# A fused encoder step: gelu and silu as single ScalarE functions, 48 loads moved to another queue, two streams of side work at other steps

## The chip, the cores and the metric

The kernel runs on one core of one Trainium2 chip. A core has five engines with their own instruction streams: TensorE (PE in the profile; its weight loads stand apart as PEld), VectorE (DVE), ScalarE (ACT), GpSimd (POOL) and SyncE (SP, which here only issues DMAs). Each engine works off its own stream in order; semaphores tie the streams together. The metric is the device time of one launch, in microseconds, as the median of several runs.

## The reference, cut to what matters

One layer of an encoder for 2048 frames of a new stream and 64 frames of a running one, 2112 token columns in all, in float32. Two branches are merged, and a feed-forward part with a short convolution follows:

```python
xn = rmsnorm(x, norm_mix);  proj = xn @ w_in          # 1024 -> 5632
x_rnn, y_gate, q, k, v, g_rnn, g_attn = split(proj)
xc = causal_dwconv(x_rnn)                             # width 4
h  = rg_lru(xc)                                       # gates, scan over positions
y_rnn  = h * gelu(y_gate)                             # jax's gelu: the tanh form
y_attn = band_attention(rope(q), rope(k), v, sinks)   # window of 128, chunks of 64
x = x + (sigmoid(g_rnn) * y_rnn + sigmoid(g_attn) * y_attn) @ w_out
up = rmsnorm(x, norm_ffn) @ w_up                      # 1024 -> 2 * 2816
gate, val = split(causal_dwconv(up))                  # width 3
x = x + (silu(gate) * val) @ w_down                   # 2816 -> 1024
y = rmsnorm(x, norm_final)                            # and the new caches and states
```

## The kernel before, in words

Data lies transposed: 128 channels on the partitions, tokens along the columns. All matrix products are made of three passes over a split operand: a float32 value is cut into a rounded high part (ACT, line 200 in `split`) and the remainder (DVE, sometimes POOL, line 201), and high*high, high*low and low*high are accumulated in PSUM. So each 128x128 piece of weights costs three matmuls per block of tokens, and each operand costs an ACT and a DVE instruction.

There are four stages.

- **Recurrent and attention stage.** The tokens are cut into three sets of two blocks (320, 384 and 352 columns). For each set all 44 column groups of `w_in` are multiplied (lines 226 to 228). In set 0 the weights come raw and are split, and the parts are kept in DRAM (`wiS`); sets 1 and 2 load them ready. Per set four attention groups run, and beside each of them two of the eight channel tiles c of the recurrent branch: `rnn_x`, `rnn_y`, the gates (`rnn_gates`), `rnn_scan`, `rnn_g`, `rnn_a`. `rnn_y` takes the product for `y_gate` out of PSUM (line 584) and makes the gelu by hand: Square on ACT (586), two DVE instructions (587, 588), Tanh on ACT (589), one more on DVE (590). The factor 1/2 of the gelu is taken later, in `mix` (620). PSUM has three buffers `mm` for the products of this stage, shared with the gates.
- **Output projection.** `wout` runs over three pairs of token blocks (304, 304 and 448 columns) and eight output tiles m. Each m needs two half tiles of `w_out` (in the first pair raw and split, then stored to `woS` by POOL's queue; in the other pairs loaded from `woS` by SP's queue) and the residual rows `xres` (line 797), four buffers of which are in turn. `residual` adds the product to them and stores them by POOL's queue to `x1S` (line 815). The buffer of m+2 is that of m, so its load waits until the store of m has landed. Beside it run `mixes` (the next pair's operand, line 774) and `xprep` (line 735).
- **Up projection.** Seven products replace eight in a Strassen form; a step is one product u of one feature tile g, in one or two lanes (pairs of token blocks). There are 140 steps with two lanes of 304 columns each (called the shared stretch here), 14 steps each for pair 0 and pair 1 alone, and 77 steps with pair 2 at 448 columns. `Lane.after` takes the sums out of PSUM, runs the convolution on ACT and DVE, and two steps later `gate` makes silu by hand: Tanh on ACT (1070), one DVE instruction over all columns (1074), and one that multiplies with the value half (1076, 1079). From step 10 on, one piece of side work per step is drawn from `fill`: `xsums` (the operand sums of pair 2, to `xS`) and then `wsums` (the weight sums of feature tiles 10 and 21, to `wuS`).
- **Down projection.** Again seven products i, each over three token pairs p and 11 pieces k. The weights of product i+1 are loaded, summed and split while product i runs; `draws(i + 1)` does one of the 11 pieces. It is called at p == 1 for k 0 to 3 and at p == 2 for k 0 to 6.

The program is written in one order, and a list scheduler reorders it for each engine before it is compiled; what it gives is fixed and is shown below for the places of interest. Tiles live in hand-managed regions (`FW`, `RA`, `RE`, `FA`, `FB`, `FD`, ...), which is why the profile names those instead of tiles after the first stage.

Of the kernel before, what the change touches and what calls it, by code (L numbers as in the profile page):

```python
# [7 lines left out]
F32 = mybir.dt.float32  # L8
F32R = mybir.dt.float32r
AF = mybir.ActivationFunctionType  # L10
ALU = mybir.AluOpType
# [3 lines left out]
P = 128  # L15
# [4 lines left out]
EPS = 1e-6  # L20
GC = 0.7978845608028654
G3 = 0.044715

SETS = [[(0, 320), (320, 320)], [(640, 384), (1024, 384)], [(1408, 352), (1760, 352)]]
BN = 384
# [103 lines left out]
def kernel(ctx: ExitStack, tc: tile.TileContext, xT, w_in, w_out, w_up, w_dn, gw, pk,  # L129
                             sinks, cq, sq, ck, sk, kcT, vcT, kcn, vcn, augk, auge, ident_in,  # L130
                             yT, kpT, ksT, vpT, vsT, kc_o, vc_o, h_o, lc_o, fc_o):
    nc = tc.nc
# [216 lines left out]
    for si, blocks in enumerate(SETS):  # L349
# [206 lines left out]
        def rnn_scan(c, st):  # L556
# [8 lines left out]
            nc.vector.scalar_tensor_tensor(a, a, 2.0, tr, op0=ALU.subtract, op1=ALU.mult)  # L565
            nc.scalar.activation(t, t, AF.Sqrt)
            nc.vector.scalar_tensor_tensor(t, t, -1.0, a, op0=ALU.mult, op1=ALU.mult)
            nc.vector.tensor_tensor(ti, ti, t, op=ALU.mult)
            nc.vector.tensor_scalar(a, a, -2.0, -1.0, op0=ALU.mult, op1=ALU.add)
            h = tr  # L570
# [6 lines left out]
        def rnn_y(c, st):  # L577

            w = kept(20 + c, si)
            st["y"] = []  # L580
            for t0, n in blocks:
                ps = proj(w, t0, n)
                y = rp_.tile([P, BN], F32, name="y")[:, :n]
                nc.scalar.activation(y, ps[:, :n], AF.Copy)
                v = rp_.tile([P, BN], F32, name="v", bufs=1)[:, :n]
                nc.scalar.activation(v, ps[:, :n], AF.Square)
                nc.vector.tensor_scalar(v, v, G3, 1.0, op0=ALU.mult, op1=ALU.add)
                nc.vector.tensor_tensor(v, v, y, op=ALU.mult)
                nc.scalar.activation(v, v, AF.Tanh, scale=GC)
                nc.vector.scalar_tensor_tensor(y, v, 1.0, y, op0=ALU.add, op1=ALU.mult)  # L590
                st["y"].append(y)
                yield
# [200 lines left out]
    def wout(i, m):  # L793
        work = []
        for t0, n in phases[i]:
            xr = io[i].tile([P, n], F32, name="xres")
            nc.sync.dma_start(xr, xT[m * P:(m + 1) * P, t0:t0 + n])
            work.append((t0, n, xr, acc()))
# [180 lines left out]
    class Lane:  # L979
# [86 lines left out]
        def gate(self):  # L1066

            n, g, p = self.n, self.g, self.p
            th = self.Gg[:, :self.cols]
            nc.scalar.activation(th, self.ug, AF.Tanh, scale=0.5)  # L1070
            h = up["c"].tile([P, 2 * n], F32, name="hp", bufs=4 if n < BM else 3)

            def mult():
                nc.vector.scalar_tensor_tensor(th, th, 1.0, self.ug, op0=ALU.add, op1=ALU.mult)
                cut = min(TP - self.t0, 2 * n)
                nc.vector.scalar_tensor_tensor(h[:, :cut], th[:, :cut], 0.5, self.uv[:, :cut],
                                               op0=ALU.mult, op1=ALU.mult)
                if cut < 2 * n:
                    nc.vector.scalar_tensor_tensor(h[:, cut:], th[:, cut + 2:], 0.5, self.uv[:, cut + 2:],
                                                   op0=ALU.mult, op1=ALU.mult)  # L1080

# [114 lines left out]

    dweights, dloads, dahead = {}, {}, [1]

    def fetch(j):
# [71 lines left out]
    for i, (lanes, fresh, u) in enumerate(plan):  # L1271
# [139 lines left out]
    for j, (i, p, k, ms, cs) in enumerate(seq):  # L1411
# [14 lines left out]

        if i < 6 and (p == 1 and k < 4 or p == 2 and k < 7):
            draws(i + 1)
# [176 lines left out]
```

## Time and profile before

| what | value |
|---|---|
| median of 3 runs | 3011.54 us (3001.13 to 3014.64) |
| the profiled execution | 3004.97 us, span 3003.1 us |
| busy share of the span | PE 96%, PEld 92%, DVE 72%, ACT 50%, POOL 14% |
| DMA | 595 MB, mean 198 GB/s |
| mean granted TensorE clock | 0.987 |

A row of groups reads: line, engine, operation, out<-in, shapes, count, then busy time in all and the mean of one in ns, then the idle time of the engine just before these instructions and what ended it. A row of waits reads: who waited, what for, total us, how often, the longest. A row of windows gives for a stretch of time the busy us of PE, PEld, DVE, ACT and POOL with the number of instructions, then the granted clock, the share of the DMA engines and GB/s. Matmuls overlap in the profile (each is given some 0.3 us while one starts every 0.14 us), so the number of matmuls that start per us tells more than PE's busy share.

### The profile page before, as it was taken

What the parts mean: (1) busy time and instruction counts of PE and PEld (TensorE: products, weight loads), DVE (VectorE), ACT (ScalarE), POOL (GpSimd) and SP (SyncE); (2) the same over time, 40 slices, a digit from 0 to 9 for tenths busy, and PEclk for the clock granted to TensorE, in tenths of its full rate; (3) what the DMA queues carried; (4) which work ended last, traced back from release to release, by engine and by line L of the source; (5) the groups of instructions that cost most, each with busy time, mean ns of one, the idle gap of its engine ahead of it and who ended that gap; (6) DMA issues with size and microseconds to landing.
All of it is one profiled execution on the core that took longest, in us unless ns stands there. A gap on an engine that the chain in (4) does not pass through costs nothing.

```text
span 3003.1 us, 49277 instructions
## 1 busy us (share of the span) xinstructions
PE 2873.6 (96%) x17640; PEld 2748.7 (92%) x17640; DVE 2157.2 (72%) x4258; ACT 1509.6 (50%) x3424; POOL 421.7 (14%) x607
## 2 busy tenths in 40 slices
PE   8989999999999999998899999999899999899998
PEld 7989888999998999998899989999899999899998
DVE  5398884377786288886578999888676667566766
ACT  4566662356653266664334445555544445334442
POOL 3221112000000000001111433222111111000001
PEclk9999999999999999999999999999999999999999
DMA  7875547544335634437885667555876677976653
GB/s 243 280 234 181 185 138 227 188 137 131 124 116 169 210 129 136 137 107 256 267 265 203 243 235 249 176 188 199 297 236 217 211 225 221 285 219 198 205 145 123
DMA packets 328854, 595.39 MB, mean 198 GB/s; under 512 B 37168, under 2 KB 230688, under 8 KB 311712
## 3 DMA queue, kind: packets, MB, share of 16 engines
q1 hardware_dynamic: 292640, 470.10, 49.8%
q0 software_dynamic: 35968, 122.13, 10.8%
q8 instruction: 139, 2.28, 0.3%
q14 instruction: 107, 0.88, 0.1%
HBM read 400.99 MB, written 191.64 MB: 197 GB/s over the span
## 4 chain that ended last, share of the span: by engine, by line
PE 46%; DMA 8%; issue 6%; DVE 6%; POOL 1%; ACT 1%; SPq 0%; DVEq 0%; POOLq 0%; ACTq 0%
PE mf L1002 4%; PE mf L1001 4%; PE mf L1003 4%; PE mm L226 4%; PE mm L227 4%; PE mm L228 4%; PE mf L1424 2%; PE mf L1425 2%; PE mf L1423 2%; PE mm L1003 2%; PE mm L1001 2%; PE mm L1002 2%; PE mm L1424 1%; PE mm L1425 1%; PE mm L1423 1%
## 5 line engine op out<-in xcount | busy, mean ns | idle before, releaser
L226 PE MATMUL mm<-xh,whl 128*128 128x320 f32 (+2 forms) x2112 | 688.3, 326 | 9.6 <-ACT xh L200 6.4
L227 PE MATMUL mm<-xl,whl 128*128 128x320 f32 (+2 forms) x2112 | 687.0, 325 | 9.0 <-DVE xl L201 4.9
L228 PE MATMUL mm<-xh,whl 128*128 128x320 f32 (+2 forms) x2112 | 683.7, 324 | 0.6 <-POOL whl L201 0.6
L200 ACT ACTIVATE RE<-FW 128x512 fp32r<-128x512 f32 (+2 forms) x555 | 304.4, 561 | 420.8 <-DMA FW<-hS 60.2
L201 DVE TENSOR_TENSOR RE<-FW,RE 128x512 fp32r<-128x512 f32 (+2 forms) x555 | 327.3, 603 | 162.2 <-ACT RE L200 159.9
L227 PEld LDWEIGHTS mm<-xl,whl 128*128 128x128 f32 x2112 | 399.8, 189 | 18.4 <-DVE xl L201 8.2
L226 PEld LDWEIGHTS mm<-xh,whl 128*128 128x128 f32 x2112 | 400.0, 189 | 17.0 <-ACT xh L200 8.8
L228 PEld LDWEIGHTS mm<-xh,whl 128*128 128x128 f32 x2112 | 399.9, 189 | 1.6 <-POOL whl L201 0.9
L1001 PE MATMUL mf<-RA,RE 128*128 128x304 f32 (+1 forms) x608 | 198.9, 327 | 3.5 <-DMA RE<-wuS 2.6
L1424 PE MATMUL mf<-RE 128*128 128x304 f32 (+2 forms) x616 | 197.8, 321 | 1.1 <-DVE RE L201 1.1
L1003 PE MATMUL mf<-RA,RE 128*128 128x304 f32 (+1 forms) x608 | 198.4, 326 | 0.4 <-DVE RE L201 0.4
L1423 PE MATMUL mf<-RE 128*128 128x304 f32 (+2 forms) x616 | 197.3, 321 | 0.6 <-ACT RE L200 0.6
L1002 PE MATMUL mf<-RA,RE 128*128 128x304 f32 (+1 forms) x608 | 197.9, 325 | 0.0
L1425 PE MATMUL mf<-RE 128*128 128x304 f32 (+2 forms) x616 | 196.0, 318 | 0.0
L1001 PE MATMUL mf<-RE 128*128 128x304 f32 (+1 forms) x488 | 159.6, 327 | 10.1 <-ACT FA L1048 5.0
L1002 PE MATMUL mf<-RE 128*128 128x304 f32 (+1 forms) x488 | 159.4, 327 | 0.9 <-DVE RE L201 0.9
L1003 PE MATMUL mf<-RE 128*128 128x304 f32 (+1 forms) x488 | 159.0, 326 | 0.2 <-DVE RE L201 0.2
L1037 DVE SCALAR_TENSOR_TENSOR FW<-FA,pkt,FW 128x608 f32<-128x608 f32 x176 | 146.1, 844 | 14.9 <-ACT FW L1031 14.7
L201 POOL TENSOR_TENSOR gl<-gr,gh 128x256 fp32r<-128x256 f32 x24 | 21.1, 878 | 800.2 <-ACT gh L200 664.1
L1001 PE MATMUL mm<-RE 128*128 128x304 f32 (+1 forms) x392 | 126.7, 323 | 5.5 <-ACT FA L1048 4.1
L1003 PE MATMUL mm<-RE 128*128 128x304 f32 (+1 forms) x392 | 126.0, 322 | 2.9 <-DVE RE L201 2.9
L457 ACT ACTIVATE pr<-S,nm 128x256 f32<-128x256 f32 (+1 forms) x272 | 123.4, 473 | 7.5 <-DVE nm L453 6.0
(341 smaller groups left out, 7287.3 us busy)
## 6 DMA issues: line engine op xcount, KB each, us to landing
whl<-wiS SPq DMA_DIRECT2D x88, 1024.0 KB, 5.1
RE<-wuS SPq DMA_DIRECT2D x104, 512.0 KB, 4.9
wiS<-whl SPq DMA_DIRECT2D x44, 1024.0 KB, 4.8
wuS<-RE POOLq DMA_DIRECT2D x80, 512.0 KB, 4.1
FW<-in_w_up_dram SPq DMA_DIRECT2D x158, 256.0 KB, 3.7
hS<-FA POOLq DMA_DIRECT2D x154, 152.0 KB, 3.8
FW<-hS SPq DMA_DIRECT2D x154, 152.0 KB, 3.3
wraw<-in_w_in_dram SPq DMA_DIRECT2D x44, 512.0 KB, 5.8
```

Of the source, the lines that this page charges most:

```text
L200: nc.scalar.activation(hi, src, AF.Copy)
L201: (lo_eng or nc.vector).tensor_tensor(lo, src, hi.bitcast(F32), op=ALU.subtract)
L226: nc.tensor.matmul(ps[:, :n], wh[:, c], xh[:, k, :n], start=first, stop=False)
L227: nc.tensor.matmul(ps[:, :n], wh[:, c], xl[:, k, :n], start=False, stop=False)
L228: nc.tensor.matmul(ps[:, :n], wl[:, c], xh[:, k, :n], start=False, stop=last)
L1001: nc.tensor.matmul(ps[:, :n], w[:, 0, c], x[:, k, 0], start=first, stop=False, **more)
L1002: nc.tensor.matmul(ps[:, :n], w[:, 0, c], x[:, k, 1], start=False, stop=False, **more)
L1003: nc.tensor.matmul(ps[:, :n], w[:, 1, c], x[:, k, 0], start=False, stop=last, **more)
L1037: nc.vector.scalar_tensor_tensor(uc, G[:, j:j + self.cols], col("fw", 44 * j + m), uc, op0=ALU.mult, op1=ALU.add)
L1423: nc.tensor.matmul(ps[m][:, cs], w[:, 0, c], t[:, 0], start=k == 0, stop=False)
L1424: nc.tensor.matmul(ps[m][:, cs], w[:, 0, c], t[:, 1], start=False, stop=False)
L1425: nc.tensor.matmul(ps[m][:, cs], w[:, 1, c], t[:, 0], start=False, stop=k == 10)
```

## The change

- `rnn_y` keeps only the copy out of PSUM. The gelu is one ACT instruction per block, `Gelu_apprx_tanh`, in place on the copy, written in `rnn_scan` behind the Sqrt. It gives the whole gelu, so `mix` adds without the factor 1/2.
- `gate` calls `Silu` on ACT; the DVE instruction that multiplied tanh + 1 with the gate is gone, and the multiplication with the value half has no factor.
- The residual rows of the output projection are loaded by POOL's queue.
- `fill` is driven at every second step.
- `draws(i + 1)` is called at the 11 places of a list.

```diff
@@ rnn_scan
             nc.scalar.activation(t, t, AF.Sqrt)
+            for y in st["y"]:
+                nc.scalar.activation(y, y, AF.Gelu_apprx_tanh)
             nc.vector.scalar_tensor_tensor(t, t, -1.0, a, op0=ALU.mult, op1=ALU.mult)
@@ rnn_y
                 nc.scalar.activation(y, ps[:, :n], AF.Copy)
-                v = rp_.tile([P, BN], F32, name="v", bufs=1)[:, :n]
-                nc.scalar.activation(v, ps[:, :n], AF.Square)
-                nc.vector.tensor_scalar(v, v, G3, 1.0, op0=ALU.mult, op1=ALU.add)
-                nc.vector.tensor_tensor(v, v, y, op=ALU.mult)
-                nc.scalar.activation(v, v, AF.Tanh, scale=GC)
-                nc.vector.scalar_tensor_tensor(y, v, 1.0, y, op0=ALU.add, op1=ALU.mult)
@@ mix
-                nc.vector.scalar_tensor_tensor(v, rr[:, o], 0.5, v, op0=ALU.mult, op1=ALU.add)
+                nc.vector.tensor_tensor(v, rr[:, o], v, op=ALU.add)
@@ wout
-            nc.sync.dma_start(xr, xT[m * P:(m + 1) * P, t0:t0 + n])
+            nc.gpsimd.dma_start(xr, xT[m * P:(m + 1) * P, t0:t0 + n])
@@ gate
-            nc.scalar.activation(th, self.ug, AF.Tanh, scale=0.5)
+            nc.scalar.activation(th, self.ug, AF.Silu)
...
-                nc.vector.scalar_tensor_tensor(th, th, 1.0, self.ug, op0=ALU.add, op1=ALU.mult)
                 cut = min(TP - self.t0, 2 * n)
-                nc.vector.scalar_tensor_tensor(h[:, :cut], th[:, :cut], 0.5, self.uv[:, :cut],
-                                               op0=ALU.mult, op1=ALU.mult)
+                nc.vector.tensor_tensor(h[:, :cut], th[:, :cut], self.uv[:, :cut], op=ALU.mult)
@@ the loop over the up projection's steps
-        drive(fill, 1)
+        if i % 2:
+            drive(fill, 1)
@@ the down projection
+    DRAWS = [(0, 8), (0, 10), (1, 3), (1, 8)] + [(2, k) for k in (0, 2, 3, 5, 6, 8, 9)]
...
-        if i < 6 and (p == 1 and k < 4 or p == 2 and k < 7):
+        if i < 6 and (p, k) in DRAWS:
             draws(i + 1)
```

How the instructions now stand on the engines is shown at three places.

**ScalarE in set 0, channel tile 4 of the recurrent branch**, from the splitting of the convolution's output (`xch`) to the gates (`tr`, `ti`). Before:

```order
L200 ACTIVATE xch<-xc 128x320
L584 ACTIVATE y<-mm 128x320
L586 ACTIVATE v<-mm 128x320
L589 ACTIVATE v<-v 128x320
L584 ACTIVATE y<-mm 128x320
L586 ACTIVATE v<-mm 128x320
L200 ACTIVATE whl<-wraw 128x1024
L200 ACTIVATE ph<-pt 128x512
L553 ACTIVATE tr<-mm,bah 128x320
```

Now:

```order
L198 ACTIVATE xch<-xc 128x320
L584 ACTIVATE y<-mm 128x320
L566 ACT_TABLE_LOAD
L566 ACTIVATE y<-y 128x320
L584 ACTIVATE y<-mm 128x320
L198 ACTIVATE whl<-wraw 128x1024
L566 ACTIVATE y<-y 128x320
L198 ACTIVATE ph<-pt 128x512
L551 ACTIVATE tr<-mm,bah 128x320
```

The scheduler does not put the gelu behind the Sqrt, as the program is written, but right behind the copy; a load of the function table stands in front of it, and another one in front of the next exponential. Over the whole program the order of ScalarE has 106 such loads, where it had 57.

**SyncE's queue at the start of the output projection's second pair**, and **GpSimd's queue** in the same stage. SP before:

```order
L797 DMA FW<-in_xT_dram 128x304 x6
L735 DMA FW<-x1S 128x304
L797 DMA FW<-in_xT_dram 128x304 x2
L785 DMA RE<-woS 128x2x512
L797 DMA FW<-in_xT_dram 128x304 x2
L785 DMA RE<-woS 128x2x512 x2
```

SP now:

```order
L782 DMA FW<-in_w_out_dram 128x512
L729 DMA FW<-x1S 128x304
L779 DMA RE<-woS 128x2x512 x3
L768 DMA FW<-mixS 128x448
L779 DMA RE<-woS 128x2x512
```

POOL before:

```order
L815 DMA x1S<-FW 128x304 x2
L790 DMA woS<-RE 256x1x512 x2
L815 DMA x1S<-FW 128x304 x22
L815 DMA x1S<-FW 128x448 x14
```

POOL now, at the same place:

```order
L784 DMA woS<-RE 256x1x512
L791 DMA FW<-in_xT_dram 128x304 x2
L809 DMA x1S<-FW 128x304 x2
L791 DMA FW<-in_xT_dram 128x304 x2
L809 DMA x1S<-FW 128x304 x6
L791 DMA FW<-in_xT_dram 128x304 x2
L809 DMA x1S<-FW 128x304 x2
```

The loads of the residual rows (`FW<-in_xT_dram`) stood ahead of the weight loads (`RE<-woS`) on SP; now they stand on POOL between the stores of the rows before them (`x1S<-FW`).

**VectorE at the start of the down projection**: the sums for the second product's weights (1163 and 1165 before, 1154 and 1156 now) among the last sums of the up projection (1087 to 1096 before) and the splits. Before:

```order
L1163 TENSOR_TENSOR FW<-FW 128x512
L201 TENSOR_TENSOR RE<-FW,RE 128x304
L1165 TENSOR_TENSOR FW<-FW 128x512
L1091 TENSOR_TENSOR FB<-FB 128x448
L201 TENSOR_TENSOR RE<-FW,RE 128x304
L1096 TENSOR_TENSOR FB<-FB 128x448
```

Now:

```order
L1154 TENSOR_TENSOR FW<-FW 128x512
L1083 TENSOR_TENSOR FB<-FB 128x448
L1156 TENSOR_TENSOR FW<-FW 128x512
L199 TENSOR_TENSOR RE<-FW,RE 128x304 x2
L199 TENSOR_TENSOR RE<-FW,RE 128x512
L1082 TENSOR_TENSOR FB<-FB 128x448
L1154 TENSOR_TENSOR FW<-FW 128x512
L1087 TENSOR_TENSOR FB<-FB 128x448
```

Two of the 11 pieces now stand ahead of the up projection's last sums (`FB<-FB`), where there was one between them.

More of the change, by code (lines that the diff above doesn't have):

```diff
@@ L20 @@
 EPS = 1e-6
-GC = 0.7978845608028654
-G3 = 0.044715
 SETS = [[(0, 320), (320, 320)], [(640, 384), (1024, 384)], [(1408, 352), (1760, 352)]]
@@ L1069, in gate @@
             th = self.Gg[:, :self.cols]
[L1070 removed]
+            nc.scalar.activation(th, self.ug, AF.Silu)
             h = up["c"].tile([P, 2 * n], F32, name="hp", bufs=4 if n < BM else 3)
             def mult():
[L1074 removed]
                 cut = min(TP - self.t0, 2 * n)
[L1076 to L1077 removed]
+                nc.vector.tensor_tensor(h[:, :cut], th[:, :cut], self.uv[:, :cut], op=ALU.mult)
                 if cut < 2 * n:
[L1079 to L1080 removed]
+                    nc.vector.tensor_tensor(h[:, cut:], th[:, cut + 2:], self.uv[:, cut + 2:], op=ALU.mult)
             def store(o, src):
```

## The prediction

> **What bounds the kernel now.** I read the page's busy shares first, then windows by stage, then what TensorE waited for in each of them, and last the timelines of the queues behind these waits.
>
> ```profile
> PE 2873.6 (96%) x17640; PEld 2748.7 (92%) x17640; DVE 2157.2 (72%) x4258; ACT 1509.6 (50%) x3424; POOL 421.7 (14%) x607
> ...
> 100.00:500.00 400.00, 364.86 (x2339) 345.21 (x2338) 320.34 (x649) 247.64 (x552) 91.32 (x53) 0.98 0.60 197
> 500.00:1350.00 850.00, 842.05 (x5145) 814.15 (x5145) 585.30 (x1392) 475.37 (x1112) 24.60 (x29) 1.00 0.45 148
> 1380.00:1510.00 130.00, 114.72 (x753) 111.61 (x753) 67.61 (x141) 45.28 (x96) 25.16 (x43) 0.94 0.89 296
> 1640.00:1890.00 250.00, 235.93 (x1652) 231.92 (x1651) 226.28 (x422) 128.48 (x304) 100.28 (x182) 0.99 0.69 239
> 1890.00:2080.00 190.00, 190.00 (x1364) 190.00 (x1364) 162.36 (x269) 101.08 (x234) 48.32 (x90) 1.00 0.53 183
> 2545.00:2620.00 75.00, 66.33 (x393) 60.16 (x392) 44.45 (x78) 26.90 (x58) 7.03 (x13) 1.00 0.98 295
> ```
>
> TensorE is the bound, and the change takes no matmul away. So only its gaps can be won or lost. The rows are, from above: set 0 of the recurrent stage (35 us idle of 400), sets 1 and 2 (8 of 850), the first two pairs of the output projection, the shared stretch of the up projection in two parts, and the start of the second down product (8.7 idle of 75). The two parts of the shared stretch run the same matmuls: 1364 in 190 us are 7.18 per us, and the 1652 of the first part would take 230.1 us at that rate. They took 250, so 19.9 us are lost there and nothing in the second part. These are the waits in the four places, in the same order (set 0; from 1395 on in the projection; the first part of the shared stretch; the down product):
>
> ```profile
> PE Y L479 <- DVE pl L201: 14.1, 15, 2.0
> PE mm L550 <- ACT v L586: 7.4, 6, 1.9
> PE mm L550 <- ACT tr L553: 4.6, 6, 1.1
> ...
> PE mm L805 <- DMA RE<-woS: 9.8, 4, 4.6
> PE mf L805 <- DMA RE<-woS: 3.2, 3, 1.9
> ...
> PE mf L1001 <- ACT FA L1048: 4.8, 3, 1.8
> PE mm L1001 <- ACT FA L1048: 4.1, 3, 3.1
> ...
> PE mm L1424 <- DVE RE L201: 6.9, 8, 1.7
> ```
>
> Everything else, some 2800 us, has a TensorE that finds its work ready; an edit there costs nothing as long as the other engines keep ahead.
>
> **Gelu.** These are the rows of the instructions that go, and the table loads:
>
> ```profile
> L587 DVE TENSOR_SCALAR v<-v 128x320 f32<-128x320 f32 (+2 forms) x48 | 20.4, 426 | 22.1 <-ACT v L586 21.7
> L588 DVE TENSOR_TENSOR v<-v,y 128x320 f32<-128x320 f32 (+2 forms) x48 | 28.5, 595 | 0.3
> L590 DVE SCALAR_TENSOR_TENSOR y<-v,y 128x320 f32<-128x320 f32 (+2 forms) x48 | 25.0, 520 | 6.6 <-ACT v L589 5.7
> L586 ACT ACTIVATE v<-mm 128x320 f32<-128x320 f32 (+2 forms) x48 | 22.0, 459 | 0.9 <-DVE y L590 0.7
> L589 ACT ACTIVATE v<-v 128x320 f32<-128x320 f32 (+2 forms) x48 | 24.0, 501 | 26.9 <-DVE v L588 26.8
> L566 ACT ACT_TABLE_LOAD x24 | 30.8, 1283 | 0.4
> ```
>
> VectorE loses 426 + 595 + 520 = 1541 ns per block, 73.9 us over 48 blocks, 24.7 of them in set 0's 16. ScalarE loses the Square (22.0 us); the Tanh becomes a Gelu, whose duration no row shows. Other functions on the same shapes lie within 459 and 501 ns, so I take the Tanh's own 501. The new order has 106 table loads for 57: 49 * 1.283 = 62.9 us more, 40.9 net, all in the recurrent stage. In sets 1 and 2 ScalarE is busy 475 of 850 us and the convolution, the exponentials and the next products hide the loads; if that cover were gone, the loads would fall on TensorE one by one (last rival). In set 0 it depends on the place. Here is channel tile 4, ScalarE first, then TensorE:
>
> ```profile
> 300.93 0.42 ACT L584 ACTIVATE y<-mm 128x320 f32<-128x320 f32 x1
> 301.25 0.43 ACT L586 ACTIVATE v<-mm 128x320 f32<-128x320 f32 x1
> 302.60 0.47 ACT L589 ACTIVATE v<-v 128x320 f32<-128x320 f32 x1 [0.92 <-DVE v L588]
> 302.98 0.42 ACT L584 ACTIVATE y<-mm 128x320 f32<-128x320 f32 x1
> 303.63 0.44 ACT L586 ACTIVATE v<-mm 128x320 f32<-128x320 f32 x1 [0.23 <-DVE y L590]
> ...
> 304.12 0.41 PE L550 MATMUL mm<-xch,gh 128*128 128x320 f32 x1 [1.53 <-ACT v L586]
> ```
>
> The gates wait for a PSUM buffer that the second block's Square frees at 304.07, because it must go to VectorE and back for the first block's `v`, of which there is one buffer. In the new order ScalarE runs copy (to 301.35), table load (to 302.63), Gelu (0.50, to 303.13), copy (to 303.55): the buffer is free 0.5 us sooner. Six such waits make some 3 of the 7.4 us. The gate behind it waits for `tr`; the second Gelu stands in front of it where the Square stood, so its 4.6 us stay.
>
> The 14.1 us of `Y <- pl` are VectorE's backlog: it works 320 of 400 us, from now on 296. If the wait goes like share/(1 - share), 4.0 falls to 2.8, 30%: 4 to 5 us. So I take **8 us less** here. Bounds: all three waits gone (-26); or the load in front of the gates costs in full in set 0 and nothing is won (8 tiles * 1.283 = +10). I am near the small gain because the timeline shows the wait's place.
>
> The Trainium skill (ScalarE: Activation LUTs, What ACT_TABLE_LOAD costs) gives a switch as a load of 1283 ns and a drain of 1380, and asks to batch calls by table set, which this order does not. The trace shows the first figure and not the second:
>
> ```profile
> 191.39 0.62 ACT L436 ACTIVATE D<-qr 128x512 fp32r<-128x512 f32 x1
> 192.03 1.28 ACT L566 ACT_TABLE_LOAD   x1
> 193.32 0.74 ACT L566 ACTIVATE t<-t 128x640 f32<-128x640 f32 x1
> ```
>
> The instruction before ended at 192.01 and the next began 0.01 us behind the load. By the skill's figure the buffer above would come 0.9 us later than before, and the sum would be some 8 us higher; I go by the row.
>
> **Silu.**
>
> ```profile
> L1074 DVE SCALAR_TENSOR_TENSOR FA<-FA,FW 128x608 f32<-128x608 f32 x44 | 34.1, 783 | 1.7 <-ACT FA L1070 1.7
> L1074 DVE SCALAR_TENSOR_TENSOR FB<-FB 128x898 f32<-128x898 f32 x22 | 24.0, 1091 | 0.0
> ```
>
> 58.1 us of VectorE go; the Tanh becomes a Silu of the same shape (I take the same time), and no table load is added in the up projection by the new order. In the shared stretch that is 0.783 us per lane and feature, in 84 matmuls or 11.7 us: 0.067 of VectorE's time.
>
> **The side work.** `xsums` has 40 pieces, the two `wsums` 8 each; with the drawing that finds each empty that is 59 steps, from step 10 to 68, and 59 * 24 / 7.18 = 197 us at the clean rate plus the 20 lost: the lost stretch has just this length. At every second step it ends at step 127, still ten steps (33 us) before the first load of its weights. VectorE's share is 0.855 in the second part and 226.28 / 230.1 = 0.983 per clean us in the first: the side work is 0.13. Halved it is 0.065, and with silu's 0.067 off VectorE stands at 0.855 + 0.065 - 0.067 = 0.853, as in the part that loses nothing. I take **18 of the 19.9 us**; the bounds are 20 and 6 (the third that silu alone gives: 0.067 of the 0.13 + 0.067 that come off, where the halved work only stretches the same waits).
>
> **Residual rows.** 48 loads leave SP. What they did to it:
>
> ```profile
> SPq L797 <- DMA x1S<-FW: 35.9, 13, 6.4
> ...
> 1425.49 8.54 SPq L797 DMA_DIRECT2D FW<-in_xT_dram  x5
> 1437.23 0.56 SPq L785 DMA_DIRECT2D RE<-woS  x1
> ...
> L815 POOL DMA_DIRECT2D x1S<-FW x46: 539/542/667, 1403.5 to 1592.0; - x46
> ...
> DMA to landing us min/median/max: 2.1/4.2/6.5
> ```
>
> SP stood 35.9 us (from 1440 on) behind residual loads that waited for a store, and the weight loads from `woS` queued behind them; TensorE's 13.0 us of waits for `woS` are these. `mixS` and `x1S` loads stay ahead of some, so I take **8 us less**, with 13 as the one bound. On POOL the wait holds up the next stores: per m two store issues, a landing, two load issues. From the first store's issue that is 4.2 + 2 * 0.54 = 5.3 us against 48 / 7.18 = 6.7 us of matmuls per m, and a row comes some 9 us after its buffer's store (two landings and an issue) where two m, 13 us, are allowed. At the longest landing it is 7.6, 0.9 too long, times 16 m: +14, the other bound. Issuing itself adds 48 * 0.54 = 26 us to a POOL that is busy 25 of 130.
>
> **Draws.**
>
> ```profile
> 2515.00:2530.00 15.00, 15.00 (x82) 14.03 (x82) 14.06 (x23) 11.96 (x30) 0.54 (x1) 1.00 0.62 179
> 2590.00:2605.00 15.00, 10.47 (x62) 8.93 (x61) 10.61 (x19) 5.78 (x13) 1.60 (x3) 1.00 1.06 312
> ```
>
> The DMA engines have room at 2515 and none at 2590, where TensorE waits for splits of late tiles. Two of the 11 pieces move forward into the first pair and the rest spreads over 9 more steps' worth, but the bytes are the same and VectorE is full (14.06 of 15) where two pieces go. I take **4 of the 8.6 us of waits**; bounds -8.6 and +4 (two pieces delaying tokens of the first product by about 2 us each; the longest wait in the row is 1.7).
>
> **Sum:** -8 - 18 - 8 - 4 = -38, on the profiled execution's 3004.97 us: 2967. The median of the runs is 6.6 us above that execution; I take part of it: **2969 us**.
>
> **Rivals.**
> 1. *The side work keeps its waits, stretched.* Against it: the second part's zero at the share I work out. For it: ScalarE's copies (L1048) wait for single VectorE instructions, and bursts may do as well. Gain 38 - 12 = 26: 2981. Chance 0.13.
> 2. *The DMA engines, not the queues, limit the output projection and the down product.* Their share is 0.89 and 0.98 there. Then 12 of the 38 go: 2981. The Trainium skill's rule that issuing engines are not separate DMA queues (DMA: Bandwidth & Descriptors) says just this; the 35.9 us are waits for semaphores, though, which it does not cover. Chance 0.17.
> 3. *POOL's queue becomes the chain of the output projection*, +14 for -8: 2991. It decides from a landing of 5.6 us on; the median is 4.2. Chance 0.05; together with 1 and 2, no change, 0.05.
> 4. *Table loads on TensorE's path (slower).* ScalarE also empties PSUM; with three `mm` buffers a product group has 24 matmuls of some 0.15 us, 3.5 us, to spare. If ScalarE falls behind by that at every switch, 62.9 us come on top in place of the 8: 3005 + 63 - 30 = 3038. Against it: the 24 loads for Sqrt and those behind them stand there now and sets 1 and 2 lose 8 us in all. Chance 0.05.
> 5. That the edits do not reach the machine is excluded for the queues by the order; a gelu in other places than written is what I costed.
>
> **How the numbers follow.** The forecast has 0.50, within 12 us of it; 0.05 is for more (all of the bounds: 2942). Range 2942 to 2997: it leaves out rivals 4 and the combined one and a part of 3. What can be told from no change is 0.5%, 15 us: below 2996 counts as faster, which the forecast and rivals 1 and 2 and most of 3 are: 0.86; same 0.09, slower 0.05.
>
> **What would show it.** In the shared stretch 7.1 matmuls per us throughout. In set 0 no wait on `v`, shorter `Y <- pl`. In the projection no wait for `woS` over 2 us, and POOL's stores at most a few us behind the sums. At the down product's second piece fewer waits for splits. It is wrong if table loads appear ahead of TensorE's waits in sets 1 and 2, or if a new wait for the residual sums (L814) appears.

## The result, and the profile after

The changed kernel takes 3027.59 us (median; 3014.18 to 3039.05), the kernel before beside it 3009.61 us (3001.13 to 3019.91). The ratio is 1.0055, with a 95% interval from 1.0038 to 1.0072: slower by half a per cent, where 1.4% less was predicted. The profiled execution took 3021.46 us, 16.5 more than the one of before.

These are the busy line of the page after and its windows by stage, the same five stages as before and the start of the second down product, which now lies some 15 us later:

```profile
PE 2876.6 (95%) x17640; PEld 2765.8 (92%) x17640; DVE 2053.2 (68%) x4048; ACT 1555.0 (51%) x3425; POOL 452.2 (15%) x655
```

```profile
100.00:500.00 400.00, 368.38 (x2365) 351.34 (x2365) 302.68 (x606) 265.41 (x556) 94.61 (x53) 0.97 0.61 201
500.00:1350.00 850.00, 839.49 (x5151) 818.30 (x5150) 550.00 (x1300) 507.70 (x1113) 25.80 (x29) 1.00 0.45 146
1380.00:1510.00 130.00, 110.81 (x727) 107.95 (x726) 62.66 (x130) 42.52 (x90) 40.03 (x70) 0.93 0.84 278
1640.00:1890.00 250.00, 235.56 (x1641) 234.06 (x1639) 210.77 (x397) 122.05 (x295) 97.35 (x178) 0.97 0.66 228
1890.00:2080.00 190.00, 187.86 (x1337) 187.61 (x1336) 153.01 (x256) 103.07 (x240) 49.92 (x92) 0.99 0.54 189
2545.00:2630.00 85.00, 75.14 (x460) 71.04 (x459) 51.97 (x93) 32.41 (x69) 10.11 (x19) 0.98 0.94 281
```

VectorE did become lighter, by 104 us over the program. In the first part of the shared stretch it works 210.77 us in place of 226.28, and yet TensorE gets through no more matmuls there, 1641, where it did 1652 (and 1644 in a second profiled execution of the kernel before); in the part behind it 1337 for 1364 (1365 in that execution). These are the waits of TensorE after, in the places that the prediction speaks of (set 0; the output projection; 1640 to 1890 us of the shared stretch; the second down product):

```profile
PE Y L477 <- DVE pl L199: 13.8, 10, 2.7
PE mm L548 <- ACT tr L551: 3.5, 3, 1.5
PE mm L224 <- ACT xh L198: 3.2, 4, 1.7
...
PE mm L548 <- ACT y L584: 2.0, 2, 1.4
...
PE mm L799 <- DMA RE<-woS: 8.1, 3, 4.1
PE mf L799 <- DMA RE<-woS: 6.9, 3, 3.1
...
PE mf L995 <- ACT FA L1042: 7.5, 2, 4.7
PE mm L995 <- ACT FA L1042: 5.9, 3, 3.9
...
PE mm L1417 <- DVE RE L199: 7.8, 6, 2.4
PE mf L1417 <- DVE RE L199: 2.0, 1, 2.0
```

Of the waits that were to go, only the one on `v` in set 0 is gone (7.4 us; 2.0 for the copy stand in its place). The others are still there. In the shared stretch the waits for the copies out of PSUM are no longer six of 1.5 us on average, but five of 2.7. Where the time lies is seen when the same matmul is looked up in both traces. The table gives the time from the first matmul of a stage to the first of the next (the last row to the end); "again" is a second profiled execution of the kernel before, and the last columns are experiments from below:

| stage, us | before | again | after | silu_only | silu_pad | silu_kept |
|---|---|---|---|---|---|---|
| start and set 0 | 450.9 | 456.2 | 449.8 | 452.4 | 448.6 | 451.3 |
| sets 1 and 2 | 923.6 | 922.5 | 920.0 | 921.7 | 924.5 | 921.2 |
| output projection | 212.8 | 212.7 | 218.0 | 211.0 | 210.8 | 208.7 |
| up projection, steps 0 to 9 | 42.5 | 45.1 | 48.4 | 42.8 | 42.9 | 42.4 |
| steps 10 to 139 (shared stretch) | 455.1 | 456.1 | 460.5 | 459.5 | 455.5 | 446.2 |
| pairs 0 and 1, one lane each | 59.8 | 59.3 | 65.8 | 65.9 | 60.4 | 61.0 |
| pair 2 | 378.0 | 378.3 | 375.7 | 382.1 | 376.9 | 376.8 |
| down projection and end | 476.8 | 478.3 | 477.9 | 480.6 | 476.1 | 476.6 |

Two executions of one program differ by up to 5 us in a stage, so a difference of that size in a single profile proves nothing; what is said below rests on the timed runs, and on what several kernels have in common.

### The profile page after: what moved, and what is told of

It is laid out like the page before. It is cut to its first block, busy times and chain, and to the rows that moved or that the text cites. A ratio compares the mean times of both kernels' runs of the same rounds, so it can differ in the third digit from the quotient of the medians.

```text
span 3019.7 us, 49053 instructions
## 1 busy us (share of the span) xinstructions
PE 2876.6 (95%) x17640; PEld 2765.8 (92%) x17640; DVE 2053.2 (68%) x4048; ACT 1555.0 (51%) x3425; POOL 452.2 (15%) x655
## 4 chain that ended last, share of the span: by engine, by line
PE 59%; issue 14%; DVE 11%; DMA 10%; POOL 3%; ACT 2%; SPq 1%; POOLq 0%; DVEq 0%; ACTq 0%
PE mm L225 8%; PE mm L226 8%; PE mm L224 8%; PE mf L1417 3%; PE mf L1418 3%; PE mf L997 3%; PE mf L1416 3%; PE mf L996 3%; PE mf L995 3%; DMA FW<-mixS 2%; PE mm L995 2%; PE mm L996 2%; PE mm L997 2%; PE mm L1417 1%; PE mm L1418 1%
## 5 line engine op out<-in xcount | busy, mean ns | idle before, releaser
L224 PEld LDWEIGHTS mm<-xh,whl 128*128 128x128 f32 x2112 | 401.9, 190 | 16.5 <-ACT xh L198 10.4
L1031 DVE SCALAR_TENSOR_TENSOR FW<-FA,pkt,FW 128x608 f32<-128x608 f32 x176 | 147.8, 847 | 17.1 <-ACT FW L1025 16.8
L455 ACT ACTIVATE pr<-S,nm 128x256 f32<-128x256 f32 (+1 forms) x272 | 122.8, 464 | 14.3 <-DVE nm L451 14.1
```

The costliest lines, as they stand in the source:

```text
L224: nc.tensor.matmul(ps[:, :n], wh[:, c], xh[:, k, :n], start=first, stop=False)
L1031: nc.vector.scalar_tensor_tensor(uc, G[:, j:j + self.cols], col("fw", 44 * j + m), uc, op0=ALU.mult, op1=ALU.add)
```

## The experiments

All times are medians beside the kernel before on the same chip; before itself lay between 3006.6 and 3009.6. The ratio, with its interval, is what is compared; it is not the quotient of two medians and can differ from it by 0.1%.

| kernel | us | ratio | 95% interval |
|---|---|---|---|
| gelu_only | 3001.48 | 0.9986 | 0.9971 to 1.0002 |
| silu_only | 3020.39 | 1.0043 | 1.0027 to 1.0059 |
| xres_only | 3019.23 | 1.0041 | 1.0021 to 1.0060 |
| fill_only | 3016.03 | 1.0023 | 1.0008 to 1.0038 |
| draws_only | 3004.17 | 0.9995 | 0.9983 to 1.0007 |
| early_loads | 3019.48 | 1.0042 | 1.0026 to 1.0058 |
| silu_pad | 3005.92 | 0.9991 | 0.9978 to 1.0004 |
| after_v2 | 3025.40 | 1.0046 | 1.0031 to 1.0061 |
| before_v2 | 3008.91 | 0.9995 | 0.9985 to 1.0005 |
| silu_skip | 3019.56 | 1.0037 | 1.0023 to 1.0051 |
| all_but_moves | 3010.55 | 1.0004 | 0.9991 to 1.0018 |
| silu_kept | 3001.69 | 0.9981 | 0.9968 to 0.9995 |
| pad_siluorder | 3035.18 | 1.0096 | 1.0077 to 1.0115 |
| all_kept | 2995.16 | 0.9955 | 0.9939 to 0.9971 |
| xres_kept2 | 3016.59 | 1.0033 | 1.0019 to 1.0047 |
| fill_kept | 3024.00 | 1.0062 | 1.0045 to 1.0079 |

**The parts alone.** Each takes one piece of the diff.

> The kernel before with the gelu edit alone. By the stages of the two traces the recurrent stage gained 0.8 us in set 0 and 3.6 in set 1, and lost 0.1 in set 2. Theory 'parts add' (each stage's loss belongs to the edit that touches it): -4 us against before, nothing after 1350 us. Rival 'table loads stand in TensorE's path': +10 or more. Rival 'a reshuffle' (the loss is not tied to an edit, any edit moves waits about): some us in stages that the edit does not touch.

> The kernel before with the silu edit alone: 66 VectorE passes, 58 us, gone. Theory 'late loads' (VectorE, working in order, stands at the side work's own loads; how much else it has to do matters little): the shared stretch gains at most 6 us of the 20 that it loses, and VectorE's waits for x1S stay at 10.6 us or grow. Rival 'VectorE's load' (the forecast's): the stretch gains 6 or more, total -6 to -10, and its waits for x1S stay the same.

> The kernel before with the residual rows' loads on POOL's queue alone. Theory 'POOL's queue holds the stores back': the output projection is 5 us longer (the difference of the two traces there: +1.9, +3.3, +0.1 for the three phases), waits for woS stay at 13 to 15 us. Rival 'the DMA engines limit the stage, whichever queue': 0 to within 2 us. The forecast's step: -8.

> The kernel before with the side work of the shared stretch at every second step alone. Theory 'late loads': each piece still stands at its own load, and the waits that it makes on TensorE are as long or longer and come over twice the steps; +8 to +17 us, nearly all of the loss. Rival 'the loss is of other edits': 0, or the gain of some 10 us that the forecast's term for the side work alone would give.

> The kernel before with the down product's pieces drawn at other steps alone. Theory 'fewer but longer waits': the waits for splits at the second down product go from 8 of at most 1.7 us to fewer of over 2, the sum stays at 8 to 9 us, total -1 to +2. The forecast's step: -4.

Gelu may gain a little (its interval just reaches 1), the draws do nothing that can be told, and the three others lose, silu too, which only takes work away. In per cent the five add to 0.88; together they cost 0.55.

> The kernel before once more, unchanged, for its profile: how far a stage's time and the half-clock time differ between two executions of one program. Theory: stages differ by up to 2 us, the time at half clock by up to 15 us, and the 448-column stage of pair 2 by 0 or 7.5 us. If a stage differs by 5 us or more elsewhere, differences of that size between two kernels' profiles show nothing.

It took 3013.91 us, and its stages stand in the table above. Its set 0 is 5 us longer than in the first profile, and no two other stages differ by 3.

**Two remedies that did not help.** The first: VectorE works its rows in order and stands at a side load that SP issued late; then more steps between load and use should help. One of the four places:

```
                     nc.sync.dma_start(x[o], x1S[kk, :, t + c0:t + c0 + width])
                 yield
+                yield
+                yield
```

> The kernel before, with extra steps inside the side work at one place only: between the issue of its loads and VectorE's first use of them (three steps for one; two for the weights' pieces), and one more between its last stores and the next loads. The work itself, silu and gelu stay as before. Theory 'late loads' (VectorE, in order, stands at a load that SP issued late behind the weights' loads, and the sum that empties PSUM stands behind it): VectorE's waits for x1S and w_up, 10.6 + 3.5 us, fall below 4, TensorE's waits for the copy out of PSUM with them, and the shared stretch gains 5 to 12 us. Rival 'VectorE's load': the same work is done, so only its stretching counts, and since the kernel with the side work at every second step lost 7 us, this is 0 to +5.

It was 0.42% slower. That does not clear late loads of blame, because this edit too moves other rows about (see the end of this section). The second: both lanes share one tile for a copy (`V`), which ties ScalarE to VectorE's addition.

```
-            if u in (0, 1) or u == 2 + (one and self.second_lane):
+            own = one and self.second_lane and "v" in up
+            if u in (0, 1) or u == 2 + (one and self.second_lane and not own):
...
+                up["v"] = Pool(FW)
+                up["v"].reserve("V", BS)
```

> The changed kernel with one thing more: the second lane's copy of X (V) gets a buffer of its own and is made at the third product, as the first lane's, where both lanes shared one buffer and the second lane's copy stood until VectorE had added the first lane's. In all ten profiles taken so far TensorE's waits in the shared stretch stand at one place, the second lane's fifth product, which accumulates into the PSUM bank that this copy reads: 8 to 11 us in sum in the kernels that are not slower there, 16.4 to 19.8 us in silu_only, fill_only, early_loads and the changed kernel. Theory 'the shared copy' (VectorE, in order, stands at a side load or a store ahead of that addition, ScalarE's copy stands behind it, TensorE behind that): the waits at this place fall from 16.6 us to under 4, with half-clock time behind them; 12 to 20 us less than the changed kernel, 3008 to 3015. Rival 'VectorE's loads hold up TensorE by any way': the waits move to the next place (the seventh product), under 5 us in all.

> The kernel before with the same own buffer for the second lane's copy. Theory 'the shared copy': the 8 to 10 us at the second lane's fifth product go, 6 to 10 us less than before. Rival as above: 0 to -3.

> The kernel with silu alone, the buffer still shared, and the side work at every step but the third of a feature, which is the one directly ahead of the addition that frees the shared copy. Theory 'the shared copy': what stands ahead of the addition matters, not how much VectorE works; the waits at the second lane's fifth product fall from 16.7 us to under 8, total 8 to 12 us less than silu_only's 3020. Rival 'in-order waits of one step earlier reach just as far': 15 or more stays.

In the same 250 us, TensorE's waits of after_v2 stand at another place and are as long in sum:

```profile
PE mf L995 <- DVE FA L1050: 10.0, 6, 2.6
PE mm L995 <- DVE FA L1050: 5.7, 3, 2.8
```

With the own buffer alone (before_v2) nothing changes either, 0.9995. The copy was where the lateness showed, not where it came from. Leaving the side work out of one step (`if u != 2: drive(fill, 1)`) did not help either.

> The edits that did not lose alone (gelu, the draws), silu, and the own buffer for the second lane's copy; the residual rows back on SP, the side work at every step. If the four parts add as measured alone (gelu -4 to -7, draws 0 to -4, silu without its loss 0 or a small gain, the own buffer -6 to -10), 2990 to 3000: ahead of both kernels. Rival: silu's loss has another cause, then 3005 to 3012.

With silu in it, nothing is left of what gelu gains.

**The pass put back.** This kernel has silu, and a VectorE pass without effect where silu saves one:

```
             def mult():
+                nc.vector.scalar_tensor_tensor(th, th, 1.0, th, op0=ALU.mult, op1=ALU.max)
                 cut = min(TP - self.t0, 2 * n)
```

> The kernel before with the silu edit and, in the place of the VectorE pass that it saves, another of the same shape that changes nothing (1.0 * th, then the maximum with th). Theory 'a lighter VectorE is slower' (it only comes sooner to its waits for loads and stores, and TensorE's waits gather into fewer, longer ones): back to before, within 3 us. Rival 'ScalarE's Silu costs': stays at +12. Rival 'chance of the state of the last 448-column stage' (that stage ran at 202.7 ns per matmul in one profile and 206.7 in another, 7.5 us in all): +7 or 0, as that stage's rate falls.

It is back at the time of before: 58 us more of VectorE's work make the program 14 us faster than silu_only. The timelines of VectorE show what no count of work shows. First silu_pad, where pair 0's single lane begins at 2085.9, then silu_only, where it begins at 2090.9:

```profile
2093.43 0.47 DVE L1052 TENSOR_TENSOR FA<-mm,FA 128x304 f32<-128x304 f32 x1
...
2094.80 0.47 DVE L1054 TENSOR_TENSOR FA<-mf,FA 128x304 f32<-128x304 f32 x1
...
2098.59 0.48 DVE L1094 TENSOR_TENSOR FA<-FA 128x304 f32<-128x304 f32 x1 [0.27 <-DMA hS<-FA]
```

```profile
2098.15 0.46 DVE L1052 TENSOR_TENSOR FA<-mm,FA 128x304 f32<-128x304 f32 x1
2098.53 0.68 DVE L201 TENSOR_TENSOR RE<-FW,RE 128x512 fp32r<-128x512 f32 x1
2099.13 0.47 DVE L1093 TENSOR_TENSOR FA<-FA 128x304 f32<-128x304 f32 x1
2103.04 0.47 DVE L1093 TENSOR_TENSOR FA<-FA 128x304 f32<-128x304 f32 x1 [3.44 <-DMA hS<-FA]
2103.43 0.47 DVE L1054 TENSOR_TENSOR FA<-mf,FA 128x304 f32<-128x304 f32 x1
```

L1054 is the sum that empties a PSUM bank. In silu_pad it stands ahead of the last in-place sums of `h` (L1094, in silu_only L1093); in silu_only both stand ahead of it, and the second waits 3.44 us for a store of `h` to land. TensorE waits for the sum behind it:

```profile
2103.95 0.41 PE L1001 MATMUL mf<-RD,RE 128*128 128x304 f32 x1 [2.85 <-DVE FA L1054]
```

The program gives both in the same order; it is the scheduler that placed them differently. A piece of VectorE's built order in the shared stretch says the same (`-` silu_pad, `+` silu_only; L935 is the side work's first use of its load, L1052 and L1054 empty PSUM):

```
 L1052 TENSOR_TENSOR FA<-mf,FA 128x304
-L201 TENSOR_TENSOR RE<-FW,RE 128x512 x2
+L935 SCALAR_TENSOR_TENSOR FA<-FA,pkt 128x224
+L201 TENSOR_TENSOR RE<-FW,RE 128x512
 L1052 TENSOR_TENSOR FA<-mm,FA 128x304
-L1085 TENSOR_TENSOR FA<-FA 128x304 x2
-L1054 TENSOR_TENSOR FA<-mf,FA 128x304 x2
-L935 SCALAR_TENSOR_TENSOR FA<-FA,pkt 128x224 x4
+L1084 TENSOR_TENSOR FA<-FA 128x304 x2
+L201 TENSOR_TENSOR RE<-FW,RE 128x512
+L1054 TENSOR_TENSOR FA<-mf,FA 128x304
+L935 SCALAR_TENSOR_TENSOR FA<-FA,pkt 128x224 x3
+L1054 TENSOR_TENSOR FA<-mf,FA 128x304
```

From the output projection to the end of the up projection, silu puts 510 of 1404 VectorE rows at another place in the order, 301 of 1260 on ScalarE, 126 of 436 on POOL and 76 of 525 on SP, as counted in the built programs. (In the traces, where rows of the same form cannot be told apart, 427 of 1395 VectorE rows are seen at another place.) silu_pad moves none, nor do gelu_only and draws_only there.

**The order put back.** To tell the order from the lighter engine, these kernels note the instructions of four queues as the program gives them, and tie each behind the one that stands ahead of it in another kernel's built order:

```
+        for one, two in zip(row, row[1:]):
+            tc.add_manual_dep(ins_of(said[two]), ins_of(said[one]).name, info, reason="order kept")
```

> The kernel with silu alone, and edges between the instructions of each of VectorE's, ScalarE's, POOL's and SP's queues, so that they stand in the up projection in just the order of the kernel before (the 64 passes that silu saves left out). Theory 'the order' (the scheduler, for which VectorE now has room, puts sums and side work that wait for a DMA ahead of the sums that empty PSUM): the 12 us that silu lost are gone; 3000 to 3010. Rival 'a lighter VectorE comes sooner to the same waits': 3017 to 3023, as silu_only.

> The reverse: silu_pad, with the pass put back in the place of the one that silu saves, but its queues in the order that silu_only has (each pass directly ahead of the product that it belongs to). VectorE has as much to do as before. Theory 'the order': 3016 to 3026, as slow as silu_only or slower. Rival 'a lighter VectorE': 3003 to 3010.

The traces show that the edges did what they were for: on all four queues the rows of silu_kept stand as in before, and those of pad_siluorder as in silu_only. Both times came out as the order would have it, and pad_siluorder was slower still than expected. The window from 1640 to 1850 us, in which most of the side work lies, of silu_pad, silu_only, silu_kept and pad_siluorder:

```profile
1640.00:1850.00 210.00, 197.29 (x1378) 193.72 (x1378) 188.52 (x356) 104.46 (x246) 84.83 (x155) 0.99 0.67 236
```

```profile
1640.00:1850.00 210.00, 194.80 (x1361) 192.56 (x1360) 176.59 (x337) 101.45 (x243) 85.31 (x155) 0.98 0.68 239
```

```profile
1640.00:1850.00 210.00, 203.01 (x1434) 201.12 (x1433) 185.70 (x355) 112.22 (x265) 89.47 (x162) 0.99 0.70 244
```

```profile
1640.00:1850.00 210.00, 189.28 (x1287) 184.25 (x1287) 180.41 (x340) 93.62 (x226) 83.60 (x153) 0.98 0.64 225
```

The lighter VectorE in the old order: 1434 matmuls, 56 more than silu_pad, or 7.8 us at 0.139 us each. The heavy VectorE in silu's order: 91 fewer. The same lighter VectorE in its own order has 17 fewer, which alone proves nothing, as the two executions of before differ by 14 here (1383 and 1397). These are single profiles, and silu_kept's was the fastest of its 12 executions, pad_siluorder's the slowest of its 5; all_kept below, whose profile was the slowest of its 7, has 1444 in this window. What decides is the timed runs: silu is worth 5 to 6 us (0.9981), and the order that the scheduler made of it cost 19 (3020.39 to 3001.69).

TensorE's waits from 1640 to 1890 us say the same, silu_only and then silu_kept (where lines are shifted, and L62 stands for most instructions of the four queues):

```profile
PE mm L1001 <- ACT FA L1048: 8.3, 3, 4.4
PE mf L1001 <- ACT FA L1048: 7.2, 4, 2.5
```

```profile
PE mf L1095 <- DVE FA L62: 4.6, 2, 3.1
PE mf L1095 <- ACT FA L62: 1.7, 3, 1.0
```

VectorE's own waits for transfers, over the up projection's steps with 304 columns, follow the order and not its work: 60.7 us in silu_only and 53.4 in pad_siluorder, 37.4 in silu_kept, 37.0 in silu_pad and 35.8 in before.

Two things remain open. A part of the 19 us may be chance: pair 2 ran at the slower of two rates in the profiles of silu_only and pad_siluorder (382.1 and 382.3 us) and at the faster in silu_pad and silu_kept (last section), and how often the timed runs had either cannot be seen. And the kernel before with edges in its own order was not run; that edges as such make a kernel faster is unlikely, since pad_siluorder has them and is the slowest of all, and xres_kept2 below has them and stays at 1.0033 for 1.0041.

> Gelu, silu and the draws together, with the four queues in the order of before from the output projection to the end of the up projection. Theory 'the order': gelu's 4 to 7 us and the draws' 0 to 4 come off and silu costs nothing or gains up to 4; 2992 to 3003, below both kernels. Rival: no better than gelu alone with silu's loss on it, 3010 to 3015.

Gelu, silu and the draws in the old order take 2995.16 us, 0.45% less than the kernel before and the lowest time measured here. The residual rows and the side work stand as before in it.

**The two other losers.**

> The residual rows' loads on POOL alone, with VectorE's, ScalarE's and SP's queues in the order of before from the output projection to the end of the up projection (there the edit moves 54, 32 and 19 rows); POOL's own order is free. Theory 'the order': the 10 us at the output projection's end and the up projection's first ten steps go, 3005 to 3011. Rival 'POOL's queue and the DMA engines': 3016 to 3022 stays.

What ran under this name was the kernel of xres_only once more, so it says nothing on the order; it is a second measurement of xres_only (3019.90, ratio 1.0041). The kernel that was meant is the next:

> The residual rows' loads on POOL alone, with VectorE's, ScalarE's and SP's queues in the order of before from the output projection to the end of the up projection (there the edit alone moves 54, 32 and 19 rows); POOL's own order is free. Theory 'the order': the 10 us at the output projection's end and in the up projection's first ten steps go, 3005 to 3011. Rival 'POOL's queue and the DMA engines': 3016 to 3022 stays.

0.33% slower in place of 0.41: the order is at most a small part here. POOL's waits at 1380 to 1600 us in xres_only, then in before, where it waited for the sums that it stores, and the median landing of the weights' loads from 1395 to 1600 us in before, then in xres_only:

```profile
POOL FW L797 <- DMA x1S<-FW: 64.7, 16, 8.0
POOL x1S L815 <- DVE FW L814: 60.5, 19, 7.9
```

```profile
POOL x1S L815 <- DVE FW L814: 137.6, 23, 12.6
```

```profile
RE<-woS SPq DMA_DIRECT2D x32, 512.0 KB, 5.4
```

```profile
RE<-woS SPq DMA_DIRECT2D x32, 512.0 KB, 6.8
```

And SP's, at 1380 to 1600 us, behind the residual loads in before and at its longest in xres_only:

```profile
SPq L797 <- DMA x1S<-FW: 55.0, 25, 6.4
```

```profile
SPq L735 <- DVE FW L747: 24.9, 4, 11.4
```

The 55.0 us that SP stood in this window are now 64.7 us that POOL stands (53.0 in the second profile of the same program), with the stores of the next rows behind. SP is none the freer: all its waits in the window add to 138.1 us in before and to 168.3 in xres_only, where it stands longer at the loads of `xprep` (L735, 59.6 us for 20.8) and `mixes` (L774, 64.8 for 40.1). In xres_kept2 TensorE's waits for `woS` did shrink, from 13.0 to 7.6 us (9.3 in xres_only):

```profile
PE mm L905 <- DMA RE<-woS: 5.3, 3, 2.6
...
PE mf L905 <- DMA RE<-woS: 2.3, 3, 1.3
```

(In the kernels with a kept order the lines are shifted.) What is won there is lost elsewhere, and one profile does not show where: the two profiles of xres_only's program differ by 12.8 us, and xres_kept2's profiled execution is 6 us under its median. Whether POOL's standing or the fuller DMA engines cost the 10 us stays open.

> The side work at every second step alone, with all rows that are not of the side work in the order of before, on VectorE, ScalarE, POOL and SP (the edit alone moves 224, 130, 54 and 13 of them against each other); the side work's rows may stand where the scheduler puts them. Theory 'the order': the 7 us that fill_only lost go, 2998 to 3008. Rival 'a side load stands ahead of a sum wherever it is put': 3012 to 3018 stays.

Slower than fill_only, so this order of the other rows is no cure. A part of it is made by the experiment: one load of raw weights now stands behind the freely placed side loads, and VectorE and TensorE wait for it once (L62 again stands for most instructions):

```profile
DVE FW L62 <- DMA FW<-in_w_up_dram: 9.9, 2, 9.6
```

```profile
PE mm L1105 <- DVE FA L62: 7.1, 1, 7.1
```

Without these 7.1 us, read from one profile, it would stand near fill_only's time. Here is the stretch that had no side work in before and has it with every second step, before and then fill_only:

```profile
1850.00:2060.00 210.00, 207.96 (x1488) 207.57 (x1489) 182.35 (x306) 112.81 (x263) 57.55 (x106) 1.00 0.56 193
```

```profile
1850.00:2060.00 210.00, 199.25 (x1418) 197.53 (x1417) 180.90 (x313) 111.59 (x267) 60.71 (x109) 1.00 0.58 200
```

70 matmuls fewer, 9.8 us (50 fewer against the second execution of before, which has 1468), while 1640 to 1850 won little: 1403 for 1383 and 1397. VectorE is no busier there than it was in before without side work, and TensorE waits all the same; early_loads, which spreads the side work too, lost 9.4 us in the same steps (69 to 139). That speaks against a cost by VectorE's share and for one by where the rows of the side work stand, but no run shows the second: the one that held the other rows in place was no faster. How much is the scheduler's (fill_only moves 224 and early_loads 227 of 1372 VectorE rows that are not side work) was not separated.

## Why the prediction was wrong, point by point

- **Silu and the side work (-18, the largest term): wrong in sign, and this is the step that failed.** The step read TensorE's waits off VectorE's busy share ("0.853, as in the part that loses nothing") and took for granted that the rows stay in their order. The share did fall, to 210.77 of 250 us and 153.01 of 190, 0.84 and 0.81, and TensorE waited all the same. What stands ahead of the prediction shows the built order at three places; the up projection, where the largest term lay, is not one of them, and there silu moves 510 rows. With the order held, silu alone gives 5 to 6 us; the lower bound of 6 for "silu alone" was the right size, under a condition that was not stated. The other half, the side work at every second step, lost 7 us; why is not shown. Rival 1 (the waits stay, stretched, and 6 of the 18 us are won) came nearest, but it did not see that the order would change, and the waits grew.
- **"Everything else" was said to cost nothing; it did not hold.** Pairs 0 and 1 with one lane each went from 59.8 to 65.8 us. All four profiles that have silu's order or the changed kernel's there (silu_only, after, after_v2, pad_siluorder) take 65.7 to 67.0, all others 57.7 to 63.6. The first ten steps of the up projection went from 42.5 to 48.4 us; there the traces range from 42.4 to 51.3, with 50.1 in all_kept, and what sets it was not found.
- **Residual rows (-8): wrong, +10 to +12.** The step that failed is that SP would be free for the weights' loads: it waited longer than before in sum, and TensorE's 13.0 us of waits for `woS` were 15.0 in the changed kernel. The 35.9 us on record for SP are those of 1440 to 1560 us alone. The bound of +14 was rival 3's, with a chance of 0.05. Its mechanism is seen in part (POOL stands 64.7 us), though the landings of the 152 KB stores stayed at 4.3 to 5.0 us in the median, under its 5.6. Rival 2 is seen as well (weights' loads 5.4 to 6.8 us). The Trainium skill's rule that DMAs run on the same DMA engines whichever engine starts them (DMA: Bandwidth & Descriptors, Issuing engines are not separate DMA queues) agrees with the landings: the same loads on another queue did not make room for the weights' loads, which took 6.8 us for 5.4.
- **Gelu (-8): sign right as far as it can be told, half the size.** 0.9986 is 4 us. The wait on `v` is gone as worked out; `Y <- pl` was to fall from 14.1 to about 9.5 and is 13.8, although VectorE's work fell from 320.34 to 302.68 us. The law share/(1 - share) did not hold; what the wait follows instead was not looked for. And the gain is not where it was forecast: over the 5 profiles with gelu against the 15 without, set 0 takes 450.7 us in the mean for 451.9, which their scatter of 1.2 to 1.9 us hides, and sets 1 and 2 take 920.6 for 923.5, with a scatter of 1.3 to 1.4. So most of it came in sets 1 and 2, where the prediction looked for none, and that the sign was right is in part luck.
- **Table loads (rival 4): did not happen.** ScalarE works 507.70 us in sets 1 and 2 for 475.37, and the two sets take 920.0 us for 923.6.
- **Draws (-4): nothing that can be told** (0.9995); the split waits are 9.8 us after for 8.6 (7.8 in draws_only, 7.7 in the second execution of before).
- **Rival 5** looked for edits that do not reach the machine. The opposite happened: more reached it than was written.

The prediction named a new wait for the residual sums (L814) as a sign of error. The wait is there after (17.0 us, four times, VectorE at L808 for the residual rows), but it is not new: before, VectorE waited 12.8 us at L814 for them, also four times. It says little either way.

## What to carry to other kernels

Where a scheduler orders the queues, taking work off an engine is two changes: the work, and a new order for everything around it. Compare the built orders of all queues in every stage on which a term of the prediction rests, and look for rows that wait for a transfer and now stand ahead of rows that TensorE waits for. If the saving is real and the time is not, put the old order back by edges before giving the saving up.

## What the runs showed of the hardware

- **TensorE's granted clock falls to a half behind pauses of some 2 us and more.** In silu_only TensorE pauses for 4.39 us from 1709.3; the windows ahead of it, of the 3.4 us behind, and after that show the granted clock in the third column from the end:

```profile
1702.00:1709.00 7.00, 7.00 (x52) 7.00 (x51) 6.11 (x13) 3.01 (x7) 4.79 (x9) 1.00 0.77 254
1714.00:1717.40 3.40, 3.40 (x16) 3.40 (x17) 3.17 (x7) 1.20 (x4) 3.06 (x7) 0.57 0.93 347
1717.50:1724.00 6.50, 6.50 (x49) 6.50 (x48) 6.50 (x14) 3.43 (x9) 1.22 (x3) 1.00 0.46 173
```

  16 matmuls in 3.4 us where 24 would fit. Over the 20 traces of this case, from the output projection on, take the pauses that have no other of over 0.4 us within 5 us of them. (A pause is the time from one matmul's start to the next, less 0.14 us.) Those of 0.4 to 1.75 us, 194 of them, were never followed by such a stretch; of those of 1.75 to 2.0 us 4 of 30 were, of 2.0 to 2.25 us 12 of 21, of 2.5 to 2.75 us 32 of 37, and of 3.5 us and more 31 of 32. So two waits of 1.5 us that stand apart are cheaper than one of 3, and that is one way in which fewer, longer waits cost time. From the up projection's first step to the end of pairs 0 and 1 the clock is halved for 17.1 us in before, silu_pad and silu_kept, for 23.4 in silu_only, 30.7 in pad_siluorder and 41.0 in the changed kernel. The Trainium skill (TensorE: Matmul & The Clock Gate, Why this matters for your kernels) asks to avoid pauses over some 3 us between bursts of matmuls; here the limit lies near 2.
- **Pair 2's matmuls of 448 columns have two steady rates, at full clock and with no waits.** The same 300 us in before, then in gelu_only, whose program is the same there:

```profile
2200.00:2500.00 300.00, 300.00 (x1482) 278.07 (x1481) 201.30 (x284) 139.01 (x338) 32.97 (x62) 1.00 0.69 220
```

```profile
2200.00:2500.00 300.00, 300.00 (x1453) 272.51 (x1452) 195.85 (x278) 134.80 (x327) 33.24 (x62) 1.00 0.69 216
```

  202.4 or 206.5 ns for a matmul; a stage keeps its rate to its end, 7 us for pair 2. The profiles of gelu_only, silu_only, fill_only, after_v2 and pad_siluorder had the slow one, the other 15 the fast one, among them after, which has the edits of the first three. What sets it stays open.
